# A substitution's rows loaded in four transfers of 32 partitions, a scheduler's DMA prices, and another admission order

## The chip, the cores and the metric

The kernel runs on one core of a Trainium2 chip. The core's engines are TensorE (PE; its weight loads are shown apart as PEld), VectorE (DVE), ScalarE (ACT), GpSimd (POOL) and SyncE (SP), which here issues every DMA of the kernel. Each engine works through its own list of instructions in order and waits on semaphores for the others. The metric is device time in microseconds (us), from three executions, with one more execution under the profiler.

## The reference

One decoder layer: a prompt of 2048 tokens and 8 single-token samples, model width 1024, everything in fp32. One input projection (1024 to 11280 columns) feeds a gated DeltaNet branch of 8 heads and a dilated attention branch of 12 heads; the branches are projected, gated, merged, projected again, normed and added to the input. What matters here is the chunked delta rule of the DeltaNet branch:

```
a_mat = jnp.where(strict, jnp.einsum('bnhcd,bnhed->bnhce', kb, k) * decay, 0.0)
u = solve(v * beta[..., None])             # (I + a_mat) u = rhs, a_mat strictly lower
w = solve(kb * jnp.exp(G)[..., None])
...
v_new = u_c - w_c @ S ; o_c = qd_c @ S + qk_c @ v_new ; S = S * gl_c + kd_c.T @ v_new   # per chunk
```

For each head and each chunk a triangular system is solved; then a state S runs from chunk to chunk.

## The kernel before, in words

The prompt is worked in two halves of 1024 tokens. In each half a main task on TensorE computes the input projection, 128 columns after another, as a block-recursive product with split operands (tiles `xs*`, `xp*` against weights `wh`, `wl`; L241 issues every matmul, L257 every transpose). Its partial sums are combined in PSUM by `to_c` and `to_d` (L974, L979), which add a bank and `etmp` on VectorE; TensorE waits for these sums. In between run the heads' tasks: short convolutions (`convw`), attention pairs, and for each of the 8 DeltaNet heads of a half the function `inverse` (L1295) and a loop over 8 chunks in `gdn` (L1150). A turn of that loop goes back and forth between TensorE and VectorE: `rr` from a product with the state `st`, `ww`, and the new `st` (the rows `rr<-bank`, `ww<-bank`, `st<-st,teGl,bank`).

`inverse` runs 16 times. The system of a head lies in a page (`at`). Its diagonal blocks of 32 x 32 are stored to DRAM (`wl_d`, four stores), and read back so that each partition holds a whole block's rows, 1024 numbers; the same 32 rows of 4 KB go to each of four groups of 32 partitions. This is `lane_w`. A second load brings the identity into `lane_t`. Then VectorE runs the substitution: 31 steps of a product (`lane_x<-lane_w,lane_t`) and a sum (`lane_t<-lane_t,lane_x`). The result goes to DRAM and back (`tl`), and products on TensorE complete the inverse. There is one set of lane buffers.

```
1307    yield K.load(wp, bass.AP(tensor=wd.tensor, offset=wd.offset, ap=[[0, 4], [1024, 32], [1, 1024]]))
1308    yield K.load(tp, I["c_consts"][:, CONST_T:])
```

No order of instructions is written down. All tasks are generators that yield operations; the class `Scheduler` keeps a clock for each engine and a table of when each buffer is written and read, and issues next the operation that can start first by its own prices (`issue`). So a price changes where every later instruction stands on its engine. A DMA is priced in `issue` (L149) by its bytes over a rate, behind the DMA that was issued before it, and `load` (L386) gives the bytes. The strings `ORDER` (L2104) say in which order the column tiles of each half are worked and admitted to the 17 pages: G adds a head's k, q and v tiles, Z its gate, a an attention tile group, g a merge gate; the other letters admit single pieces of work.

Of the kernel before, what the change touches and what calls it, by code (L numbers as in the profile page):

```python
# [86 lines left out]
class Scheduler:  # L87
# [54 lines left out]
    def issue(self, op, alt, start):  # L142
        eng, cost, fn = alt
        fn()
        end = start + cost
        self.clock[eng] = end
        self.busy[eng] += cost
        if op.nbytes:
            self.dma = max(self.dma, end + 650.0) + op.nbytes / 360.0  # L149
            end = self.dma  # L150
            eng = "dma"
        bufs = self.bufs
        for n in op.reads:
            b = bufs.setdefault(n, [0.0, 0.0, None, None])
            if end > b[1]:
                b[1], b[3] = end, eng
        for n in op.writes:
            b = bufs.setdefault(n, [0.0, 0.0, None, None])
            if end > b[0]:
                b[0], b[2] = end, eng  # L160
# [40 lines left out]
def _names(*aps):  # L201
    return tuple(a.tensor.name for a in aps if isinstance(a, bass.AP))


def _free(ap):
    n = 1
    for x in ap.shape[1:]:
        n *= x
    return n


class Ops:
# [10 lines left out]
    def mm_cost(self, out, lhsT, rhs):  # L223
        n = _free(rhs)
        if lhsT.dtype == F32R:
            return max(n / 2.215, 107.0)
        k, m = lhsT.shape[0], _free(lhsT)
        floor = 214.0 if m > 64 else (125.0 if m > 32 else 77.0)
        return max(n * 1.68, floor)
# [31 lines left out]
    def act_alt(self, out, in_, func, scale=1.0, bias=0.0, accum_out=None):  # L261
        nc = self.nc
        c = _free(in_) / 1.2 + (51.0 if self.in_psum(in_) else 93.0)
        c += 93.0 * (isinstance(scale, bass.AP) + isinstance(bias, bass.AP) + (accum_out is not None))
        if accum_out is not None and func == AF.Square:
            c += 130.0
        kw = dict(scale=scale, bias=bias)
        if accum_out is not None:
            kw["accum_out"] = accum_out
        return ("act", c, lambda: nc.scalar.activation(out, in_, func, **kw))  # L270
# [115 lines left out]
    def load(self, out, in_):  # L386
        nc = self.nc
        n = 4 * _free(out) * out.shape[0]
        return Op([("sp", 475.0, lambda: nc.sync.dma_start(out, in_))], _names(in_), _names(out), nbytes=n)  # L389


# [51 lines left out]
def build(nc, tc, ctx, I, O):  # L443
# [7 lines left out]
    K = Ops(nc, {b.tensor.name for b in banks})  # L451
# [698 lines left out]
    def gdn(hf, h, tk, tq, tv, tz, work, done):  # L1150
# [43 lines left out]
        for u in range(2):  # L1194
# [8 lines left out]
            side.release(b)  # L1203
        U_ev, Q_ev, V_ev = Event(), Event(), Event()
        S.spawn(inverse(at, U_ev), 11, f"inv{h}")
        S.spawn(gdn_q(tq, kT, e, gp, sm, tb, h, Q_ev), 12, f"gq{h}")
        qT, qk = yield Wait(Q_ev)
# [87 lines left out]
    def inverse(at, ev):  # L1295

        i = gidx[0] % 3
        gidx[0] += 1
        wd, td = wl_d[i], tl_d[i]
        a3 = at[:, :HT].rearrange("p (n c) -> p n c", c=128)  # L1300
        wv = wd.rearrange("(n b) (j i) -> b j n i", b=4, i=32)
        for b in range(4):
            yield K.load(wv[b], a3[32 * b:32 * b + 32, :, 32 * b:32 * b + 32])

        ln = yield Acquire(lanes, 1)
        wp, tp, xp = ln
        yield K.load(wp, bass.AP(tensor=wd.tensor, offset=wd.offset, ap=[[0, 4], [1024, 32], [1, 1024]]))
        yield K.load(tp, I["c_consts"][:, CONST_T:])
        W = wp.rearrange("p (j i) -> p j i", i=32)
        Tm = tp.rearrange("p (c i) -> p c i", i=32)  # L1310
        for j in range(31):
            m = 31 - j
            x = xp[:, :8 * m].rearrange("p (c i) -> p c i", i=m)
            yield K.tt(x, W[:, j, None, j + 1:].to_broadcast([128, 8, m]),
                       Tm[:, :, j, None].to_broadcast([128, 8, m]), OP.mult)
            yield K.tt(Tm[:, :, j + 1:], Tm[:, :, j + 1:], x, OP.add)
        yield K.load(td, tp)
        lanes.release(ln)
        tb, pt = yield Acquire(prob_t, 2)
        TB = tb.rearrange("p (n c) -> p n c", c=64)  # L1320
        Uv = a3
        yield K.pset(TB[0:32, :, 32:64], 0.0)
        tv = td.rearrange("(q n b) (c i) -> b q c n i", q=4, b=4, i=32)
        for b in range(4):
            for q in range(4):
                r = 32 * b + 8 * q
                yield K.load(Uv[r:r + 8, :, 32 * b:32 * b + 32], tv[b, q])
        for b in range(4):
            yield K.vtr(TB[32 * b:32 * b + 32, :, 32 * (b % 2):32 * (b % 2) + 32],
                        Uv[32 * b:32 * b + 32, :, 32 * b:32 * b + 32])  # L1330
        P1 = pt[:, :256].rearrange("p (n c) -> p n c", c=32)
        bank = yield Acquire(side, 1)
        b1 = bank[:, :256].rearrange("p (n c) -> p n c", c=32)
        b2 = bank[:, 256:].rearrange("p (n c) -> p n c", c=32)
        for a in range(2):
            lo, hi = slice(64 * a, 64 * a + 32), slice(64 * a + 32, 64 * a + 64)
            yield K.mms([(b1[hi, n], a3[lo, n, 64 * a + 32:64 * a + 64], TB[lo, n, 0:32], True, True)
                         for n in range(8)])
            yield K.copy(P1[hi], b1[hi])
        yield K.mms([(b2[32:64, n], Uv[32:64, n, 32:64], P1[32:64, n], True, True) for n in range(8)])  # L1340
        for a in range(2):
            lo, hi = slice(64 * a, 64 * a + 32), slice(64 * a + 32, 64 * a + 64)
            yield K.mms([(b2[lo, n], P1[hi, n], Uv[hi, n, 64 * a + 32:64 * a + 64], True, True) for n in range(8)])
        yield K.copy(TB[32:64, :, 0:32], b2[32:64])
        for a in range(2):
            lo = slice(64 * a, 64 * a + 32)
            yield K.copy(Uv[lo, :, 64 * a + 32:64 * a + 64], b2[lo])
        side.release(bank)
        bank = yield Acquire(side, 1)
        b1 = bank.rearrange("p (n c) -> p n c", c=64)  # L1350
        yield K.mms([(b1[64:128, n], a3[0:64, n, 64:128], TB[0:64, n], True, True) for n in range(8)])
        P2 = pt.rearrange("p (n c) -> p n c", c=64)
        yield K.copy(P2[64:128], b1[64:128])
        yield K.mms([(b1[0:64, n], P2[64:128, n], Uv[64:128, n, 64:128], True, True) for n in range(8)])
        yield K.copy(Uv[0:64, :, 64:128], b1[0:64])
        side.release(bank)
        prob_t.release(tb, pt)
        ev.set(at)
# [731 lines left out]
    def conv_state():  # L2090
# [10 lines left out]
    plan, admits = [], []  # L2101


    ORDER = ("GZaaGaaGZaagZGaZagGZaagGagZaGaZaggGaZaggggggxgggyg",  # L2104
             "gGZgaagGagZSaggGaZaGagZagGaagTZGaZaCgggGaaZgGZaggag")
    for hf in range(2):
        tiles = []

# [45 lines left out]

        for what in ORDER[hf]:
            if what in "GZag":
# [5 lines left out]
            else:  # L2162
                ev, n = {"S": (sg_admit, 4), "T": (sat_admit, 3), "C": (cs_admit, 1)}[what]
# [101 lines left out]
def trace(nc, arrays):  # L2265
    from contextlib import ExitStack

    ins = {n: nc.dram_tensor(f"in_{n}", a.shape, mybir.dt.from_np(a.dtype), kind="ExternalInput").ap()
           for n, a in arrays.items()}
    outs = [nc.dram_tensor(f"out_{i}", s, F32, kind="ExternalOutput").ap() for i, s in enumerate(_OUTS)]  # L2270
    with tile.TileContext(nc) as tc, ExitStack() as ctx:
        return build(nc, tc, ctx, ins, outs)
# [13 lines left out]
```

## Time and profile before

| | |
|---|---|
| median of 3 executions | 3112.87 us (3108.63 to 3118.22) |
| profiled execution | 3111.94 us, span of its instructions 3110.2 us |
| mean granted TensorE clock | 0.988 |
| PE busy | 3028.9 us, 97% of the span |
| DVE busy | 2193.5 us, 71% |
| ACT busy | 1218.4 us, 39% |
| DMA queue of SP | 331.49 MB, 36.3% of 16 engines' time |

PE is busy nearly all the time, so a change in this kernel is read from what interrupts PE: an idle stretch and what ended it, and the granted clock, which is shown as a share of 2.4 GHz and has the two levels 1.0 and 0.5. A wait is put down to the instruction or the DMA that came last before it ended.

### The profile page before, as it was taken

What the parts mean: (1) busy time and instruction counts of PE and PEld (TensorE: products, weight loads), DVE (VectorE), ACT (ScalarE), POOL (GpSimd) and SP (SyncE); (2) the same over time, 40 slices, a digit from 0 to 9 for tenths busy, and PEclk for the clock granted to TensorE, in tenths of its full rate; (3) what the DMA queues carried; (4) which work ended last, traced back from release to release, by engine and by line L of the source; (5) the groups of instructions that cost most, each with busy time, mean ns of one, the idle gap of its engine ahead of it and who ended that gap; (6) DMA issues with size and microseconds to landing.
All of it is one profiled execution on the core that took longest, in us unless ns stands there. A gap on an engine that the chain in (4) does not pass through costs nothing.

```text
span 3110.2 us, 55704 instructions
## 1 busy us (share of the span) xinstructions
PE 3028.9 (97%) x20879; PEld 2702.7 (87%) x20879; DVE 2193.5 (71%) x5975; ACT 1218.4 (39%) x3427; POOL 131.0 (4%) x237
## 2 busy tenths in 40 slices
PE   7999999989999999999999999999999999999999
PEld 6999999989999999978877778888888888898887
DVE  6767866776868478666676757686978686766765
ACT  4544444434444343433433434343424443222121
POOL 1000000000000000000000000000000000000000
PEclk9999999999999999999999999999999999999999
DMA  4222232232323225322233232236453225565463
GB/s 120 77 66 80 68 88 82 81 88 67 89 72 86 73 87 150 105 72 79 71 100 107 80 107 85 81 90 181 138 146 99 77 75 160 170 227 191 140 238 115
DMA packets 434135, 335.06 MB, mean 108 GB/s; under 512 B 62313, under 2 KB 377201, under 8 KB 433856
## 3 DMA queue, kind: packets, MB, share of 16 engines
q1 hardware_dynamic: 433864, 331.49, 36.3%
q8 instruction: 164, 2.69, 0.4%
q14 instruction: 107, 0.88, 0.1%
HBM read 253.01 MB, written 80.97 MB: 107 GB/s over the span
## 4 chain that ended last, share of the span: by engine, by line
PE 82%; DVE 8%; DMA 8%; SPq 1%; issue 1%; ACT 1%; POOL 0%; DVEq 0%; POOLq 0%; ACTq 0%
PE bank L241 78%; PE bank L257 4%; DMA lane_t<-in_c_consts 3%; DVE pg L301 2%; SPq L389 1%; DVE wl L306 1%; DMA pg<-og 1%; DVE lane_x L306 1%; DVE lane_t L306 1%; DMA wr<-in_w_in 1%; DMA pg<-sq_d 1%; DMA pg<-in_state_gdn 1%; DMA wl<-pg 0%; DVE pg L306 0%; DVE wh L345 0%
## 5 line engine op out<-in xcount | busy, mean ns | idle before, releaser
L270 ACT ACTIVATE pg<-bank 128x256 f32<-128x256 f32 (+8 forms) x755 | 341.5, 465 | 762.9 <-PE bank L241 681.5
L306 DVE TENSOR_TENSOR wl<-wr,wh 128x512 fp32r<-128x512 f32 x595 | 383.7, 647 | 20.6 <-ACT wh L270 3.6
L241 PE MATMUL bank<-xp7s,wh 128*128 128x512 f32 (+3 forms) x1196 | 305.4, 330 | 0.0
L345 DVE CAST wh<-wr 128x512 fp32r<-128x512 f32 (+1 forms) x377 | 150.3, 399 | 219.0 <-PE bank L241 195.0
L241 PE MATMUL bank<-xp6s,wh 128*128 128x512 f32 (+3 forms) x1132 | 289.0, 331 | 0.0
L270 ACT ACTIVATE wh<-wr 128x512 fp32r<-128x512 f32 (+1 forms) x220 | 134.2, 611 | 382.9 <-PE bank L241 325.0
L241 PE MATMUL bank<-xp5s,wh 128*128 128x256 f32 (+3 forms) x1100 | 278.4, 330 | 0.0
L241 PE MATMUL bank<-xp4s,wh 128*128 128x260 f32 (+2 forms) x1068 | 267.5, 327 | 0.0
L306 DVE TENSOR_TENSOR bank<-bank,etmp 128x256 f32<-128x256 f32 (+2 forms) x260 | 134.8, 519 | 135.7 <-PE bank L241 132.0
L241 PEld LDWEIGHTS bank<-xp7s,wh 128*128 128x128 f32 x1196 | 199.8, 189 | 17.3 <-issue 1.5
L241 PEld LDWEIGHTS bank<-xp6s,wh 128*128 128x128 f32 (+1 forms) x1132 | 188.9, 188 | 17.0 <-DVE xp6s L301 0.2
L241 PEld LDWEIGHTS bank<-xp5s,wh 128*128 128x128 f32 (+1 forms) x1100 | 183.3, 189 | 15.3 <-issue 0.8
L241 PE MATMUL bank<-xp7s,wl 128*128 128x512 f32 (+3 forms) x592 | 195.7, 331 | 0.0
L241 PEld LDWEIGHTS bank<-xp4s,wh 128*128 128x128 f32 x1068 | 176.1, 188 | 14.2 <-issue 1.5
L306 DVE TENSOR_TENSOR lane_x<-lane_w,lane_t 128x248 f32<-128x248 f32 (+30 forms) x496 | 141.8, 286 | 64.3 <-DMA lane_t<-in_c_consts 58.2
L241 PE MATMUL bank<-xp6s,wl 128*128 128x512 f32 (+2 forms) x560 | 185.9, 332 | 0.0
L301 DVE SCALAR_TENSOR_TENSOR pg<-pg,convw,pg 128x1024 f32<-128x1024 f32 x144 | 184.0, 1278 | 1.9 <-issue 0.5
L241 PE MATMUL bank<-xp5s,wl 128*128 128x512 f32 (+2 forms) x544 | 178.5, 328 | 0.0
L241 PE MATMUL bank<-xs1k,wh 128*128 128x512 f32 (+4 forms) x708 | 178.1, 335 | 0.0
L241 PE MATMUL bank<-xs6k,wh 128*128 128x512 f32 (+3 forms) x680 | 174.3, 335 | 0.3 <-DVE xs6k L306 0.3
L241 PE MATMUL bank<-xp4s,wl 128*128 128x256 f32 (+2 forms) x528 | 173.7, 329 | 0.0
L241 PE MATMUL bank<-xs7k,wh 128*128 128x512 f32 (+3 forms) x680 | 172.3, 335 | 0.0
(297 smaller groups left out, 7428.4 us busy)
## 6 DMA issues: line engine op xcount, KB each, us to landing
wr<-in_w_in SPq DMA_DIRECT2D x176, 512.0 KB
pg<-in_x_prompt SPq DMA_DIRECT2D x32, 512.0 KB
wr<-in_w_proj_a SPq DMA_DIRECT2D x32, 512.0 KB
wr<-in_w_out SPq DMA_DIRECT2D x32, 512.0 KB
pg<-og SPq DMA_DIRECT2D x24, 520.0 KB
pg<-gate SPq DMA_DIRECT2D x24, 512.0 KB
out<-pg SPq DMA_DIRECT2D x20, 512.0 KB
og<-pg SPq DMA_DIRECT2D x32, 260.0 KB
```

Of the source, the lines that this page charges most:

```text
L241: nc.tensor.matmul(out, lhsT, rhs, start=start, stop=stop, skip_group_check=shared)
L257: nc.tensor.transpose(out, in_, ident[:k, :k])
L270: return ("act", c, lambda: nc.scalar.activation(out, in_, func, **kw))
L301: lambda: nc.vector.scalar_tensor_tensor(out, in0, scalar, in1, op0=op0, op1=op1, **kw))],
L306: return ("dve", self._vcost(out, in0, in1), lambda: nc.vector.tensor_tensor(out, in0, in1, op=op))
L345: alts.append(("dve", self._vcost(out, in_, fast=True), lambda: nc.vector.tensor_copy(out, in_)))
L389: return Op([("sp", 475.0, lambda: nc.sync.dma_start(out, in_))], _names(in_), _names(out), nbytes=n)
```

## The change

Three edits. The load of `lane_w` becomes four loads of 32 partitions, each with the plain 32 x 1024 source. The scheduler's price of a DMA goes from 360 to 270 bytes per nanosecond, and a transfer whose contiguous runs on both sides hold at least 512 numbers has its bytes counted at 0.72 (270 / 0.72 = 375). The two strings that admit tiles are changed at some places.

```
-            self.dma = max(self.dma, end + 650.0) + op.nbytes / 360.0
+            self.dma = max(self.dma, end + 650.0) + op.nbytes / 270.0
...
+def _run(ap):
+    run = 1
+    for step, n in reversed(list(ap.ap)[1:]):
+        if step != run:
+            break
+        run *= n
+    return run
...
         n = 4 * _free(out) * out.shape[0]
+        n *= 0.72 if min(_run(out), _run(in_)) >= 512 else 1.0
...
-        yield K.load(wp, bass.AP(tensor=wd.tensor, offset=wd.offset, ap=[[0, 4], [1024, 32], [1, 1024]]))
+        for q in range(4):
+            yield K.load(wp[32 * q:32 * q + 32], wd)
         yield K.load(tp, I["c_consts"][:, CONST_T:])
...
-    ORDER = ("GZaaGaaGZaagZGaZagGZaagGagZaGaZaggGaZaggggggxgggyg",
+    ORDER = ("GZaaGaaZGaagZGaZagGaZagGagZaGaZgaggGgaZaggggxggygg",
```

The second string of `ORDER` has one pair of letters exchanged. PE, DVE, ACT and POOL get the same work as before; SP gets 1353 DMAs where it had 1305.

SP's list at the fifth of the sixteen inversions (the fifth head of the first half), before. `wl_163` is the DRAM tile with the head's blocks, `wr_*` are the two buffers for weights, `grow` is a row of decays:

```order
L389 DMA pg_98<-grow_158 128x1024
L389 DMA snew_d<-pg_106 128x8
L389 DMA wl_163<-pg_100 32x8x32 x2
L389 DMA wr_113<-in_w_in 128x8x128
L389 DMA wl_163<-pg_100 32x8x32
L389 DMA wr_112<-in_w_in 128x8x128
L389 DMA wl_163<-pg_100 32x8x32
L389 DMA lane_w<-wl_163 128x1x1024
L389 DMA lane_t<-in_c_consts 128x256
```

The same place in the change:

```order
L400 DMA pg_100<-grow_158 128x1024
L400 DMA wl_163<-pg_101 32x8x32 x2
L400 DMA snew_d<-pg_110 128x8
L400 DMA wl_163<-pg_101 32x8x32 x2
L400 DMA lane_w<-wl_163 32x1024
L400 DMA wr_113<-in_w_in 128x8x128
L400 DMA wr_112<-in_w_in 128x8x128
L400 DMA lane_w<-wl_163 32x1024 x3
L400 DMA lane_t<-in_c_consts 128x256
```

One load has become four, the identity's load stands behind all four, and at this place two weight loads stand between the first and the other three.

DVE's list at the start of the same substitution, before (`lane_x<-lane_w,lane_t` is its first product; `bank_68<-bank_66,etmp` is a sum of the projection, `pg_99<-pg_104,pg_99` the end of a convolution):

```order
L301 SCALAR_TENSOR_TENSOR pg_99<-pg_104,pg_99 128x1024
L306 TENSOR_TENSOR bank_68<-bank_66,etmp 128x256
L301 SCALAR_TENSOR_TENSOR st_146<-st_146,teGl,bank_72 128x128
L301 SCALAR_TENSOR_TENSOR rr<-bank_72,tneG,pg_110 128x128
L345 COPY ww<-bank_72 128x128
L301 SCALAR_TENSOR_TENSOR st_146<-st_146,teGl,bank_72 128x128
L306 TENSOR_TENSOR lane_x<-lane_w,lane_t 128x248
L306 TENSOR_TENSOR lane_t<-lane_t,lane_x 128x8x31
L301 SCALAR_TENSOR_TENSOR rr<-bank_72,tneG,pg_110 128x128
```

The same place in the change:

```order
L316 TENSOR_TENSOR bank_68<-bank_66,etmp 128x256
L311 SCALAR_TENSOR_TENSOR rr<-bank_69,tneG,pg_98 128x128
L355 COPY ww<-bank_69 128x128
L311 SCALAR_TENSOR_TENSOR st_146<-st_146,teGl,bank_69 128x128
L301 TENSOR_SCALAR sm_141<-sm_141 128x8
L311 SCALAR_TENSOR_TENSOR pg_99<-bank_71,ghh,pg_99 128x512
L311 SCALAR_TENSOR_TENSOR rr<-bank_69,tneG,pg_98 128x128
L311 SCALAR_TENSOR_TENSOR pg_103<-bank_70,sm_141,pg_103 128x128 x2
L311 SCALAR_TENSOR_TENSOR st_146<-st_146,teGl,bank_69 128x128
L311 SCALAR_TENSOR_TENSOR pg_103<-bank_70,sm_141,pg_103 128x128
L316 TENSOR_TENSOR lane_x<-lane_w,lane_t 128x248
L311 SCALAR_TENSOR_TENSOR pg_103<-bank_70,sm_141,pg_103 128x128
```

Behind the same sum `bank_68<-bank_66,etmp` the first product stood after the end of one turn of the chunk loop and one whole turn; now it stands after two whole turns and, on the way, five other instructions. Over the sixteen inversions DVE's list has on the mean 20 instructions between the last one that writes the head's system and the first product before, and 35 in the change.

## Rows read from the trace of the kernel before

**Rows 1.** Page, part 1: busy time, share of the span, instructions.

```profile
PE 3028.9 (97%) x20879; PEld 2702.7 (87%) x20879; DVE 2193.5 (71%) x5975; ACT 1218.4 (39%) x3427; POOL 131.0 (4%) x237
```

**Rows 2.** Waits of PE: total us, times, longest us.

```profile
PE bank L241 <- DVE rr L301: 17.7, 8, 8.6
PE bank L241 <- DMA cst<-in_c_consts: 11.3, 1, 11.3
```

**Rows 3.** Tile lane_w: duration ns min/median/max, first and last start; idle time before.

```profile
L306 DVE TENSOR_TENSOR lane_x<-lane_w,lane_t x496: 157/283/419, 135.5 to 2575.3; 128x248 f32<-128x248 f32 x6, 128x224 f32<-128x224 f32 x6, 128x200 f32<-128x200 f32 x6, 128x176 f32<-128x176 f32 x6
L389 SPq DMA_DIRECT2D lane_w<-wl x16: 539/573/621, 125.0 to 2527.1; - x16
...
  DMA lane_t<-in_c_consts: 58.2, 13
```

**Rows 4.** Timeline, DVE, fifth inversion: start us, us, instruction, [idle before <- releaser].

```profile
663.24 0.35 DVE L301 SCALAR_TENSOR_TENSOR st<-st,teGl,bank 128x128 f32<-128x128 f32 x1 [0.64 <-PE bank L241]
672.38 0.42 DVE L306 TENSOR_TENSOR lane_x<-lane_w,lane_t 128x248 f32<-128x248 f32 x1 [8.80 <-DMA lane_t<-in_c_consts]
...
673.17 0.34 DVE L301 SCALAR_TENSOR_TENSOR rr<-bank,tneG,pg 128x128 f32<-128x128 f32 x1
```

**Rows 5.** Timeline, PE, behind six starts of a substitution.

```profile
143.63 0.51 PE L241 MATMUL bank<-xs5k,wh 128*128 128x260 f32 x2 [2.81 <-DVE bank L306]
...
260.64 0.79 PE L241 MATMUL bank<-st,pg 128*128 128x128 f32 x2 [6.14 <-DVE st L301]
...
673.57 0.80 PE L241 MATMUL bank<-rr,pg 128*128 128x128 f32 x2 [8.56 <-DVE rr L301]
...
957.83 0.79 PE L241 MATMUL bank<-rr,pg 128*128 128x128 f32 x2 [5.45 <-DVE rr L301]
...
1750.83 3.54 PE L241 MATMUL bank<-pg,pg 128*128 128x2 f32 x16 [5.66 <-DMA pg<-in_state_gdn]
...
2053.19 0.49 PE L241 MATMUL bank<-rr,pg 128*128 128x128 f32 x2 [1.10 <-DVE rr L301]
```

**Rows 6.** Timeline, SP: start us, us until issued, DMAs; fifth, eighth, thirteenth inversion.

```profile
659.98 0.57 SPq L389 DMA_DIRECT2D lane_w<-wl  x1
660.60 0.47 SPq L389 DMA_DIRECT2D lane_t<-in_c_consts  x1
...
1130.59 1.80 SPq L389 DMA_DIRECT2D wl<-pg  x4
1133.72 0.58 SPq L389 DMA_DIRECT2D lane_w<-wl  x1
...
2041.77 12.37 SPq L389 DMA_DIRECT2D wr<-in_w_in  x2
```

**Rows 7.** Windows: stretch, us, busy by engine, granted clock, DMA share, GB/s.

```profile
2.00:7.00 5.00, 0.00 (x0) 0.00 (x0) 2.46 (x4) 1.28 (x1) 0.00 (x0) 1.00 0.96 343
...
534.70:538.70 4.00, 4.00 (x37) 4.00 (x36) 2.60 (x6) 2.90 (x15) 0.00 (x0) 1.00 0.26 84
1137.00:1141.00 4.00, 4.00 (x36) 4.00 (x36) 1.03 (x4) 2.06 (x11) 0.00 (x0) 1.00 0.25 80
```

**Rows 8.** Windows: PE first; stretches at the lower granted clock, each with the next.

```profile
258.30:265.10 6.80, 4.46 (x21) 4.46 (x22) 3.50 (x11) 0.21 (x1) 0.00 (x0) 0.50 0.07 24
265.10:272.00 6.90, 6.90 (x61) 6.90 (x61) 6.55 (x24) 2.91 (x13) 1.28 (x3) 1.00 0.05 12
667.90:678.10 10.20, 4.53 (x21) 4.54 (x22) 3.80 (x12) 1.63 (x8) 0.00 (x0) 0.50 0.62 95
678.10:688.30 10.20, 10.20 (x88) 10.20 (x88) 9.87 (x38) 3.38 (x12) 1.01 (x1) 1.00 0.41 121
...
1749.90:1760.10 10.20, 9.27 (x34) 8.43 (x35) 8.06 (x23) 0.00 (x0) 0.00 (x0) 0.50 0.01 3
1760.10:1770.30 10.20, 10.20 (x51) 8.31 (x50) 8.66 (x24) 6.06 (x10) 0.00 (x0) 1.00 0.24 64
```

More of the change, by code (lines that the diff above doesn't have):

```diff
@@ L2101, in build @@
     plan, admits = [], []
-    ORDER = ("GZaaGaaGZaagZGaZagGZaagGagZaGaZaggGaZaggggggxgggyg",
-             "gGZgaagGagZSaggGaZaGagZagGaagTZGaZaCgggGaaZgGZaggag")
+    ORDER = ("GZaaGaaZGaagZGaZagGaZagGagZaGaZgaggGgaZaggggxggygg",
+             "gGZaaggGagSaZggGaZaGagZagGaagTZGaaZCgggGaaZgGZaggag")
     for hf in range(2):
```

## The prediction

> **What bounds the kernel now.** I read the page's busy times first: PE is busy for 3028.9 of 3110.2 us [rows 1], so 81.3 us of its idle time are all that a change of order can give back, besides time in which PE runs at the lower clock. Next I asked what PE waits for. The largest wait with one cause is for `rr`, the row of the chunk loop that VectorE makes from PE's product, 17.7 us in 8 times [rows 2]. A row of 0.35 us cannot hold PE up for 8.6 us by itself, so the third question is what kept VectorE. The view of `lane_w` tells it: VectorE stood idle for 58.2 us in 13 times at the first product of a substitution, waiting for its loads [rows 3]. At the fifth inversion the order of events is plain. `st` ends at 663.6, the next row in VectorE's list is the first product, it begins at 672.38 after 8.80 us of idleness, and `rr` stands behind it, at 673.17 [rows 4]; PE goes on at 673.57, after 8.56 us [rows 5]. VectorE is no bound by its work (71% busy [rows 1]); it is in order, and what stands behind the waiting product is what PE needs.
>
> PE's stretches of this kind are six that I can follow: 2.81, 6.14, 8.56, 5.45, 5.66 and 1.10 us, together 29.7 [rows 5]. The first is a delay passed on (the sum in `bank` came late because VectorE began late); in the fifth PE waits for a load of `in_state_gdn` that was issued behind a `lane_w`. After four of them PE runs at granted clock 0.50, which is 1.2 GHz, for 6.8 to 10.2 us, then at 2.4 GHz again [rows 8]. What that costs I take from the work done: behind the second wait 21 matmuls took 4.46 us, and in the stretch after it 61 took 6.90, so 21 would take 2.4 and 2.1 are lost; behind the third 21 took 4.53 against 88 in 10.20, again 2.1 lost; behind the fifth 34 took 9.27 against 51 in 10.20, 2.5 lost. The fourth is like the second (1.8). Sum 8.5 us; the mix of matmuls differs between such stretches, so it is an estimate, good to some 3 us.
>
> Why are the loads late? `lane_w` was issued at 659.98 [rows 6] and was needed at 663.6, and the product began 12.4 us after the issue. Its 512 KB move slowly: in two stretches with hardly anything else under way the DMA engines are busy for 0.26 and 0.25 of their time and move 84 and 80 GB/s, while the loads of `in_x_prompt` at the start, 128 partitions of the same 4 KB rows, fill 0.96 and move 343 GB/s [rows 7]. A quarter of 16 engines is four, and four is the outer count of the load's pattern (`[0, 4]`). At 82 GB/s the 512 KB take 6.4 us, at 343 they take 1.5. The scheduler priced them at 1.5 us, and so it put the product where it had to wait. Others suffer too: two weight loads behind a `lane_w` took 12.37 us to be issued [rows 6].
>
> **The change part by part.** *The four transfers.* Each has 32 partitions outermost, rows of 4 KB. No row of before shows just this form. Bounds: it is as fast as the 128-partition load (343 GB/s), or as slow as `lane_w` was. I take the first, since the two loads differ in the outer count alone and each fits the engines it could use; halfway between would change little, as will be seen. Readiness from the first issue: four issues at 0.573 us [rows 3] and the identity's at 0.47 [rows 6] are 2.8 us, and behind the last issue there is a tail. For the tail the nearest row is that of the four stores to `wl`: the last is issued by 1132.39 and the load that waits for them starts at 1133.72, 1.3 us [rows 6]. I take 2.0 for a larger transfer, so 4.8 us in place of 12.4 at the fifth inversion, and of 10.5 at the first (125.0 to 135.5 [rows 3]).
>
> A rule of the Trainium skill speaks against this edit: "DMA: Bandwidth & Descriptors", section Rules for kernel authors, says of two transfers to disjoint partition halves that they are not worth it, since both use all 16 engines anyway, and that one 128-partition transfer is better. By that rule the time to readiness would only grow by three issues, 1.7 us, and the gain would be what the new order covers (the third rival below). The same section says that an outermost dimension below 16, a zero-stride broadcast for one, confines a DMA to that many engines; the trace agrees, with 0.25 and 0.26 of the engines' time [rows 7].
>
> *The place of the product.* Over the sixteen inversions there are 35 instructions on VectorE in place of 20 between the last one that writes the system and the first product. An instruction takes 3110.2 / 5975 = 0.52 us of VectorE's span [rows 1], so the product stands some 7.8 us later, with useful work ahead of it. Either alone, the faster load (by 5.7 us or more) or the later place, would take most of 58.2 us; with both I expect under 5 us left. What is late next? The inverse itself ends later by what the product was moved (7.8 us) less the wait that is gone (58.2 / 16 = 3.6), some 4 us a head. That costs nothing as long as PE has projection matmuls to run, and it has: outside of such waits it hardly idles [rows 1, 2].
>
> *The issues.* 48 more at 0.573 us are 27.5 us on SP, 1.7 us an inversion. Queued behind them are weight loads and the identity. Cover: the weights are loaded one column pair ahead, and no row of PE's waits names a weight. If the cover were gone at every inversion, it would cost up to 27.5 us; I take 0.
>
> *The prices and the strings.* They add and remove no work; PE gets the same matmuls. They shuffle what remains: 81.3 less the 29.7 and less 11.3 us at the start, before the constants have landed [rows 2], is 40 us of idleness for other reasons. A quarter of it either way, 10 us, is the range I give to luck; its middle is 0.
>
> *The sum.* 3111.9 (the profiled execution) less 29.7, less 8.5, is 3073.7. That execution was 0.9 us under the median of the three, so on the median's scale the forecast is 3075 us. Bounds: 3056 if the other idleness falls by 10 us and its clock losses by some 9 with it; 3102 if the issues uncovered cost 27.5.
>
> **The rivals.** *Half is given back.* The waits of these places go, and others of the 40 us kind grow, or some issues are uncovered: 3075 plus half of the 38.2 us, 3094. For it: an in-order kernel at 97% has little slack, and every instruction has moved. Against it: the six waits had one cause that is taken away, whatever the order.
>
> *The transfers are no faster* and only the order helps. Then readiness is 1.7 us later and the product 7.8 later, a relief of 6.1 us. Of the six waits 2.5 us of the third stay, and all 5.66 of the fifth, which comes from a load stuck behind `lane_w`; with two of four clock losses (4.6) that is 12.8 us kept, 3088. The rule quoted above would give this case.
>
> *No change:* what is gained at these places is lost again whole, 3104 to 3122. For it: 40 us of idleness have causes that I have not followed, and the admission order touches all of them.
>
> *Slower,* by one mechanism. SP is in order, and at the fifth inversion the list of the change puts two weight loads between the first part of `lane_w` and the other three. Such a load waits until its buffer has been split on VectorE; if it waits long, so do three parts, the identity, and the substitution, and with it the page of the head; PE then stops at the products that need the inverse. To eat the 38.2 us and end 9.3 us over before, this must cost PE (38.2 + 9.3) / 16 = 3.0 us at every inversion. Against it: there are some 8 us of VectorE's work as new cover, and readiness has 5.7 us to spare.
>
> **How the numbers follow.** I take 9.3 us (0.3%) as what a measurement of this kernel can tell from no change: the three executions of before lie within 9.6. Chances: the forecast (3060 to 3084, below 3060 included) 0.62, half given back (3084 to 3103) 0.17, transfers no faster (about 3088) 0.06, no change 0.09, slower 0.06. The first three are faster by over 0.3%: 0.85. The range of 8 in 10 leaves out the last two cases, 0.15, and a little at the low end: 3056 to 3102. The likeliest case's own range is 3060 to 3084.
>
> **What would show it.** Right: VectorE's idle time at `lane_x` falls from 58.2 to under 5 us; readiness from the first `lane_w` issue is about 5 us; DMA share right behind those issues is far over 0.25; PE's wait for `rr` falls from 17.7 to under 5 us, and the stretches at 0.50 behind substitutions are gone, so that the mean granted clock is over 0.99; PE's busy time falls by some 8 us and its idleness to about 52. Wrong: if VectorE still waits as long at `lane_x`, the transfers or their place on SP are to blame; if it does not wait there and PE is idle for 80 us all the same, the order gave it back, and the view of PE's waits names where.

## The result and the profile after

The changed kernel takes 3060.47 us (median of 4 runs, 3055.23 to 3061.43); the kernel before, run beside it, 3110.75 us (3107.09 to 3118.22). The ratio is 0.9832, with a 95% interval of 0.9809 to 0.9854: 50 us faster, where 38 were forecast. The direction and the range held, but the time lies at the lower edge of the likeliest case (3060 to 3084); two terms of the sum were too small.

The span of the profiled execution is 3059.6 us, the mean granted clock 0.992. The page's busy times, to be held against [rows 1]:

```profile
PE 3018.4 (99%) x20879; PEld 2698.0 (88%) x20879; DVE 2204.1 (72%) x5957; ACT 1216.7 (40%) x3443; POOL 131.2 (4%) x239
```

PE does the same 20879 matmuls. Its busy time is 10.5 us less, and its idle time is 3059.6 - 3018.4 = 41.2 us in place of 81.3, so 40.1 less. Together these are the 50.6 us by which the span is shorter.

The view of PE's waits after, against [rows 2] (total us, times, longest us):

```profile
PE bank L267 <- DVE pg L316: 11.5, 5, 6.4
PE bank L251 <- DMA cst<-in_c_consts: 10.3, 1, 10.3
PE bank L251 <- DVE rr L311: 1.9, 4, 1.0
```

The wait for `rr` is down from 17.7 to 1.9 us. A wait that was not among the rows of before now leads. It is for pages that VectorE writes with an elementwise operation (TENSOR_TENSOR, L316, which is L306 in the kernel before); the longest of the five, 6.4 us, stands at 35.0 us, where the kernel before waits 4.6 us for a load of `in_a_log`, and the other four stand near 1293. More of it under the experiments. The tile `lane_w` after, against [rows 3]:

```profile
L316 DVE TENSOR_TENSOR lane_x<-lane_w,lane_t x496: 163/285/419, 138.2 to 2529.4; 128x248 f32<-128x248 f32 x6, 128x224 f32<-128x224 f32 x6, 128x200 f32<-128x200 f32 x6, 128x176 f32<-128x176 f32 x6
L400 SPq DMA_DIRECT2D lane_w<-wl x64: 312/421/2547, 124.8 to 2479.6; - x64
its engine sat idle before it (us, times) until:
who waited for it (us, times):
```

There are 64 loads in place of 16, with a median issue of 0.421 us against 0.573, and the list of what VectorE waited for ahead of a product is empty: 58.2 us in 13 times became nothing. At the fifth inversion, against [rows 4], VectorE does not wait at the first product, and `rr` follows 0.6 us behind it:

```profile
666.76 0.35 DVE L311 SCALAR_TENSOR_TENSOR st<-st,teGl,bank 128x128 f32<-128x128 f32 x1
667.02 0.35 DVE L311 SCALAR_TENSOR_TENSOR pg<-bank,sm,pg 128x128 f32<-128x128 f32 x1
667.28 0.41 DVE L316 TENSOR_TENSOR lane_x<-lane_w,lane_t 128x248 f32<-128x248 f32 x1
667.61 0.34 DVE L311 SCALAR_TENSOR_TENSOR pg<-bank,sm,pg 128x128 f32<-128x128 f32 x1
667.87 0.34 DVE L311 SCALAR_TENSOR_TENSOR rr<-bank,tneG,pg 128x128 f32<-128x128 f32 x1
```

SP's timeline of the same inversion, against [rows 6] (start, us until issued, DMAs):

```profile
652.17 0.32 SPq L400 DMA_DIRECT2D lane_w<-wl  x1
652.87 3.42 SPq L400 DMA_DIRECT2D wr<-in_w_in  x2
656.34 2.06 SPq L400 DMA_DIRECT2D lane_w<-wl  x3
658.44 0.42 SPq L400 DMA_DIRECT2D lane_t<-in_c_consts  x1
```

Two weight loads did stand between the first part and the other three, for 3.42 us, and the identity was issued 6.3 us after the first part. The product at 667.28 comes 15.1 us after the first issue, and the product did not wait. The windows view, with the columns of [rows 7], shows the speed of the four transfers (ahead of two substitutions), two stretches at a lower granted clock, and the second place of the new wait:

```profile
239.80:241.30 1.50, 1.50 (x48) 1.46 (x46) 0.17 (x1) 1.20 (x2) 0.00 (x0) 1.00 0.90 249
2479.50:2481.00 1.50, 1.50 (x12) 1.34 (x10) 0.90 (x3) 0.94 (x1) 0.00 (x0) 1.00 0.91 265
...
375.00:381.80 6.80, 6.40 (x30) 5.86 (x29) 5.87 (x13) 3.28 (x9) 0.40 (x1) 0.52 0.01 2
388.00:394.80 6.80, 6.24 (x29) 5.84 (x30) 5.85 (x17) 3.65 (x15) 1.01 (x1) 0.53 0.84 218
1293.00:1303.20 10.20, 7.19 (x28) 5.57 (x29) 9.71 (x28) 3.37 (x6) 0.00 (x0) 0.50 0.35 83
```

The share of the engines is 0.90 and 0.91 in the first two, where one load alone had 0.25 and 0.26. In the last PE works for 7.19 of 10.20 us, at granted clock 0.50, which is 1.2 GHz. The stretches at 375 and 388 us are new: from 340 to 420 us the granted clock is 0.91 here and 1.00 in the kernel before.

### The profile page after: what moved, and what is told of

Same layout as the page of the kernel before. It is cut to its first block, busy times and chain, and to the rows that moved or that the text cites. A ratio compares the mean times of both kernels' runs of the same rounds, so it can differ in the third digit from the quotient of the medians.

```text
span 3059.6 us, 55757 instructions
## 1 busy us (share of the span) xinstructions
PE 3018.4 (99%) x20879; PEld 2698.0 (88%) x20879; DVE 2204.1 (72%) x5957; ACT 1216.7 (40%) x3443; POOL 131.2 (4%) x239
## 4 chain that ended last, share of the span: by engine, by line
PE 94%; DVE 4%; DMA 1%; issue 1%; ACT 1%; POOL 0%; SPq 0%; DVEq 0%; POOLq 0%; ACTq 0%
PE bank L251 89%; PE bank L267 5%; DVE pg L311 1%; DVE wl L316 0%; DVE lane_t L316 0%; DVE lane_x L316 0%; DVE pg L316 0%; DVE junk L311 0%; DMA pg<-in_x_prompt 0%; DMA wr<-in_w_in 0%; DMA ghh<-in_g_head_norm 0%; DMA pg<-gate 0%; DVE wh L355 0%; ACT L280 0%; ACT pg L280 0%
## 5 line engine op out<-in xcount | busy, mean ns | idle before, releaser
L280 ACT ACTIVATE pg<-bank 128x256 f32<-128x256 f32 (+5 forms) x738 | 333.9, 464 | 746.0 <-PE bank L251 676.9
L316 DVE TENSOR_TENSOR wl<-wr,wh 128x512 fp32r<-128x512 f32 x595 | 384.0, 647 | 20.1 <-ACT wh L280 2.2
L316 DVE TENSOR_TENSOR bank<-bank,etmp 128x256 f32<-128x256 f32 (+2 forms) x260 | 135.0, 519 | 138.3 <-PE bank L251 133.4
L251 PEld LDWEIGHTS bank<-xp6s,wh 128*128 128x128 f32 (+1 forms) x1132 | 189.0, 188 | 18.2 <-issue 1.5
L251 PEld LDWEIGHTS bank<-xp5s,wh 128*128 128x128 f32 (+1 forms) x1100 | 182.9, 188 | 15.1 <-issue 0.8
L280 ACT ACTIVATE prob<-bank 128x512 f32<-128x512 f32 (+4 forms) x221 | 102.6, 478 | 189.0 <-PE bank L251 116.2
```

Source lines behind the costliest of these rows:

```text
L251: nc.tensor.matmul(out, lhsT, rhs, start=start, stop=stop, skip_group_check=shared)
L316: return ("dve", self._vcost(out, in0, in1), lambda: nc.vector.tensor_tensor(out, in0, in1, op=op))
```

## The experiments

The theory was that the slow load held VectorE up, and with it PE, so that the speed of the load alone should give most of the gain. The rival was that the other order, made by the prices, the strings and the four operations, gave it by putting the product later or by moving something else. All ratios are to the kernel before on the same chip, with 95% intervals. Edits are against the kernel before unless a heading says otherwise.

**e1, the fast load in the old order.** One operation for the scheduler, with the old price, issues four transfers. The lists of PE, VectorE, ScalarE and GpSimd are then those of before, row for row; SP alone has 48 issues more.

```
+    def parts(self, pairs):
+        nc = self.nc
+        n = sum(4 * _free(o) * o.shape[0] for o, _ in pairs)
+        def go():
+            for o, i in pairs:
+                nc.sync.dma_start(o, i)
+        return Op([("sp", 475.0, go)], _names(pairs[0][1]), _names(pairs[0][0]), nbytes=n)
...
-        yield K.load(wp, bass.AP(tensor=wd.tensor, offset=wd.offset, ap=[[0, 4], [1024, 32], [1, 1024]]))
+        yield K.parts([(wp[32 * q:32 * q + 32], wd) for q in range(4)])
```

> The kernel before with its lists for PE, DVE, ACT and POOL unchanged row for row; only the one lane_w load on SP is issued as four of 32 partitions. Theory (the load was slow because its outer count is 4, and the faster load removes the waits by itself): readiness about 5 us after the first issue in place of 10.5 to 13.6, DVE's idle time at lane_x from 58.2 to under 6 us, time about 3075 us, a gain of 30 to 45. Rival (transfers no faster, the new order is what helped): DVE still idle for over 50 us there, time 3108 to 3140, the three more issues included.

Measured: 3057.47 us (3049.92 to 3060.85), ratio 0.9823 [0.9805, 0.9841]. The whole gain is there without a price or a string changed; the expected 3075 was too high, as the forecast was. The page's busy times, the tile `lane_w`, SP's timeline and VectorE's at the fifth inversion, one fence each:

```profile
PE 3009.4 (99%) x20879; PEld 2689.8 (88%) x20879; DVE 2193.8 (72%) x5975; ACT 1219.8 (40%) x3427; POOL 132.4 (4%) x237
```

```profile
L392 SPq DMA_DIRECT2D lane_w<-wl x64: 312/420/1512, 124.2 to 2467.1; - x64
...
  DMA lane_t<-in_c_consts: 5.3, 4
```

```profile
648.27 1.70 SPq L392 DMA_DIRECT2D lane_w<-wl  x4
650.01 0.42 SPq L398 DMA_DIRECT2D lane_t<-in_c_consts  x1
```

```profile
652.73 0.42 DVE L306 TENSOR_TENSOR lane_x<-lane_w,lane_t 128x248 f32<-128x248 f32 x1 [0.99 <-DMA lane_t<-in_c_consts]
```

The product starts as soon as its loads have landed, 652.73 - 648.27 = 4.5 us after the first issue, where one load took 12.4. PE idles for 3048.1 - 3009.4 = 38.7 us. Since the lists are equal, any wait of PE that is gone is gone by the load's speed.

**e8, e1 once more,** to know how firm it is.

> The lists of before with the load in four transfers, once more, beside the changed kernel. Theory (the new prices and strings give nothing beyond the load): within 0.3% of the changed kernel, 3050 to 3064. Rival (they cost, since the substitution is put 7 us later without need): 5 us or more below the changed kernel. Second rival (the first run of it was lucky): 5 us or more above it, as the forecast's 3075 would have it.

Measured: 3053.19 us (3050.64 to 3054.13), 0.9821 [0.9801, 0.9841]; VectorE idle at `lane_x` for 3.7 us in 4 times.

**e2, the slow load in the new order** (against the changed kernel): its lists are kept, but the first of the four operations issues the old load of all 128 partitions, and the other three issue nothing.

```
-            yield K.load(wp[32 * q:32 * q + 32], wd)
+            op = K.load(wp[32 * q:32 * q + 32], wd)
+            whole = bass.AP(tensor=wd.tensor, offset=wd.offset, ap=[[0, 4], [1024, 32], [1, 1024]])
+            go = (lambda: K.nc.sync.dma_start(wp, whole)) if q == 0 else (lambda: None)
+            op.alts = [("sp", 475.0, go)]
+            yield op
```

> The change with its lists for PE, DVE, ACT and POOL unchanged row for row; SP issues the old single load at the place of the first of the four, and nothing at the other three. In the trace after, the first product begins 12.4 to 23.7 us behind that place, the old load is ready after 9.5 to 13.8. Theory (either the faster load or the later place takes the waits away): DVE idle at lane_x under 12 us, time 3060 to 3080. Rival (the slow load also harms what stands behind it on the 16 engines and on SP, wherever the product stands): DVE does not wait at lane_x, but other loads are late, time 3080 to 3100.

Measured: 3073.42 us (3071.35 to 3074.69), 0.9872 [0.9854, 0.989]. The new order alone gives 40 us on this chip (3113.08 before), so either part alone takes most of the wait: VectorE idles for 1.3 us in 2 times. What stays is the harm to others. The lists of the four compute engines are those of the changed kernel, so what is longer here, beyond scatter, is so by the load. PE's waits in e2:

```profile
PE bank L251 <- DMA pg<-in_state_gdn: 5.9, 1, 5.9
PE bank L251 <- DVE bank L316: 4.9, 2, 3.8
```

The load of `in_state_gdn` is late again, by about as much as in [rows 5], where the changed kernel has no wait at all, and one wait for `bank` is longer by 3.8 us. e2 is 16 us over e1 on the same chip.

**e3, e1 with two transfers of 64 partitions:**

```
+        yield K.parts([(wp[64 * q:64 * q + 64], bass.AP(tensor=wd.tensor, offset=wd.offset, ap=[[0, 2], [1024, 32], [1, 1024]]))
+                       for q in range(2)])
```

> As the first run of this call, lists of before unchanged on four engines, but the load is two transfers of 64 partitions, each with the outer count 2 in its source pattern. Theory (the outer count sets how many engines move a load): two engines, DMA share near 0.13 and some 42 GB/s with nothing else under way, readiness 6 us and more later than before, DVE idle at lane_x well over 120 us, time over 3170. Rival (a load is slow for its repeated source or for its size, and smaller transfers are faster): readiness between that of four and of one transfer, time 3075 to 3112.

Measured: 3188.6 us (3185.42 to 3192.79), 1.0243 [1.0224, 1.0263], slower than before. Splitting in itself brings nothing here; the outer count decides. Three stretches with little but these transfers under way, in the windows view:

```profile
365.00:373.00 8.00, 8.00 (x74) 7.79 (x74) 5.13 (x13) 4.75 (x21) 0.00 (x0) 1.00 0.13 41
...
854.00:860.00 6.00, 6.00 (x53) 6.00 (x53) 4.48 (x12) 2.23 (x14) 0.00 (x0) 1.00 0.12 43
...
552.00:558.00 6.00, 6.00 (x53) 6.00 (x52) 4.42 (x10) 3.15 (x18) 0.00 (x0) 1.00 0.13 51
```

An outer count of two gives half the share (0.12 to 0.13) and about half the rate of four. The wait grows with it, on VectorE (tile `lane_w`) and from there on PE (its waits):

```profile
  DMA lane_t<-in_c_consts: 123.9, 15
```

```profile
PE bank L241 <- DVE rr L301: 37.4, 9, 12.8
PE bank L241 <- DVE bank L306: 28.2, 10, 7.2
```

**e9, the four loads alone.** Four operations for the scheduler, with the old prices and strings, so that the lists differ a little from before.

```
-        yield K.load(wp, bass.AP(tensor=wd.tensor, offset=wd.offset, ap=[[0, 4], [1024, 32], [1, 1024]]))
+        for q in range(4):
+            yield K.load(wp[32 * q:32 * q + 32], wd)
```

> The kernel before with four lane_w loads that the scheduler sees as four operations, at the old prices and with the old strings, so that the lists move as the scheduler decides. Theory (the load is all of the gain): 3050 to 3066 us, DVE idle at lane_x under 8 us. Rival (four operations on SP at old prices put the product or the weights at worse places): 3070 to 3095.

Measured: 3059.99 us (3057.56 to 3062.86), 0.9847 [0.9833, 0.986]; VectorE idles for 0.4 us at `lane_x`, once.

**e4, the change without its strings.**

```
-    ORDER = ("GZaaGaaZGaagZGaZagGaZagGagZaGaZgaggGgaZaggggxggygg",
-             "gGZaaggGagSaZggGaZaGagZagGaagTZGaaZCgggGaaZgGZaggag")
+    ORDER = ("GZaaGaaGZaagZGaZagGZaagGagZaGaZaggGaZaggggggxgggyg",
+             "gGZgaagGagZSaggGaZaGagZagGaagTZGaZaCgggGaaZgGZaggag")
```

> The change with the ORDER strings of before: four transfers and the new prices. Theory (the strings only shuffle; the load and its price are the gain): 3060 to 3080, DVE idle at lane_x under 5 us. Rival (the part of the gain that the forecast did not have, some 12 us, comes from the strings): 3070 to 3080 with the further idle time of PE back in the second half; or more than that, 3085 and over, if the strings carry more.

Measured: 3062.92 us (3058.67 to 3065.84), 0.9838 [0.9819, 0.9857]; VectorE idles for 1.2 us at `lane_x`, in 2 times.

**e5, the strings alone** (those two lines of the change, the one slow load).

> The kernel before with the ORDER strings of the change alone: one lane_w load of 128 partitions, old prices. Theory (the whole gain comes from the load): DVE still idle for 45 to 70 us at lane_x, time 3100 to 3125, no difference that can be told. Rival (the strings carry part of the 50 us): 3070 to 3100.

Measured: 3121.09 us (3114.23 to 3131.0), 1.004 [1.0028, 1.0052]. VectorE waits for 60.9 us in 11 times at `lane_x`, against 58.2 in 13. The time lies in the range of the theory, but its "no difference that can be told" failed: the interval leaves out 1.

**e6, the prices alone** (360 to 270, and 0.72 with `_run`; the one slow load).

```
-            self.dma = max(self.dma, end + 650.0) + op.nbytes / 360.0
+            self.dma = max(self.dma, end + 650.0) + op.nbytes / 270.0
...
+        n *= 0.72 if min(_run(out), _run(in_)) >= 512 else 1.0
```

> The kernel before with the new prices alone (270, and 0.72 for long runs): one lane_w load, which is priced at 375 bytes per ns in place of 360, old strings. Theory (the prices do not know of the outer count, so the product stays where it is): DVE idle at lane_x 45 to 70 us, time 3100 to 3125. Rival (dearer short runs move the substitution or the weights enough): DVE idle under 40 us, time 3070 to 3100.

Measured: 3097.06 us (3090.67 to 3106.61), 0.9963 [0.9949, 0.9977]; 45.6 us in 11 times at `lane_x`. The idle time is as the theory had it, the time as its rival. With the slow load the strings cost 12 us and the prices bring 12.

**e7, the changed kernel again,** on the chip of e5, e6 and e8.

> The changed kernel once more, to stand on the same chip as the next run. 3055 to 3066 us; the same shape as in its first profile, no DVE idle time at lane_x.

Measured: 3056.83 us (3053.46 to 3059.75), 0.9834 [0.9813, 0.9855].

**e10, the fast load as one operation with the new prices,** old strings: e1 and the edit of e6 together.

> Four transfers issued as one operation of the scheduler, with the new prices and the old strings: the order that the prices alone give, with the fast load. The prices alone gave 12 us without it. If these 12 us are of another kind than the load's, this is the fastest version, 3040 to 3050 us; if they came from putting waits elsewhere that the fast load removes as well, 3050 to 3064, no better than the changed kernel.

Measured: 3050.64 us (3041.43 to 3056.21), 0.9815 [0.9793, 0.9837], the lowest of all. Its interval overlaps those of e1, e8 and the change, so that it beats them is not shown. Against e9 on the same chip it is 9 us faster, and each of its 4 times is below each of the 5 of e9; the two differ in the prices and in the number of operations, and which of them does it was not tried.

What follows from the ten: with the fast load, the five kernels that differ in prices, strings and operations per load (e1 and e8, e9, e4, e10, the change) lie between 0.9815 and 0.9847, and their intervals overlap: the load is the gain, and the rest moves these medians by 10 us at most. With the slow load the prices and strings are worth some 12 us each, in opposite directions. In the profile the new prices have one visible cost. Every kernel that has them (the change, e2, e4, e6, e7, e10) shows PE waiting 10.0 to 12.5 us in 5 times for pages that VectorE writes at L316; 6.1 to 6.4 us of that are the wait at 35 us. Without the prices PE waits 4.6 to 4.8 us there, for `in_a_log`. So the prices cost some 1.5 us at the start. The rest, 3.9 to 6.4 us, stands near 1300 us (the windows row at 1293 is part of it); without the prices it is 3.0 to 3.1 us in e1, e3, e5, e8 and before, but 5.8 in e9, so that the prices are not shown to be what makes it longer.

## Why the prediction was right, and where its sizes were off

**The mechanism** (one in-order engine held by a slow load, and PE behind it) is shown by e1: nothing on the four compute engines was moved, the load was made faster, and the gain came whole.

**The speed of the four transfers.** The prediction took the rate of the 128-partition load with no row for it. The changed kernel's 0.90 of the engines' time and 249 GB/s, in a stretch that holds the beginnings and ends of the transfers too, put it on the side of that bound (343) and far from the other (82); what the sum needed, the time to readiness, came out as said below.

The rule that was weighed against this edit ("DMA: Bandwidth & Descriptors" of the Trainium skill, section Rules for kernel authors, on two transfers to disjoint partition halves) takes for granted that one transfer already uses all 16 engines. Here that didn't hold, and e1 shows a gain where the rule alone would give none. Where two transfers to disjoint halves were run, each with an outer count of two (e3), the engines were busy for 0.12 to 0.13 of their time. The other row of the same section, that a small outermost count confines a DMA to so many engines, agrees with shares of 0.12 to 0.13 for two, 0.25 to 0.26 for four and 0.90 for 32.

**Readiness** was put at 4.8 us from the first issue; e1 has 4.5 where VectorE waits for it. In the changed kernel it can't be read, as no product waits. VectorE's idle time at `lane_x` was put under 5 us and is 0. That either half alone would take most of the wait holds too: 5.3 us stay in e1 and 1.3 in e2.

**One reading was wrong, without weight in the sum.** The 12.37 us that two weight loads took to be issued were put down to the `lane_w` ahead of them. In e1, behind the fast load, the same two loads at the thirteenth inversion still take 8.68 us (1993.93 in SP's timeline), so at most 3.7 us were the load's.

**The first term that was mis-sized** is "PE's stretches of this kind are six that I can follow ... together 29.7". PE's idle time fell by 40.1 us in the changed kernel and by 42.6 in e1. The prediction had set 40 us aside as "idleness for other reasons" with a middle of 0. In equal pieces of work (the same matmuls, within three, on PE in each), the windows view of before and then of e1:

```profile
0.00:1300.00 1300.00, 1254.71 (x11018) 1236.08 (x11019) 922.49 (x2620) 584.62 (x1808) 67.74 (x136) 0.99 0.31 87
1300.00:2684.00 1384.00, 1354.82 (x7779) 1118.75 (x7778) 994.71 (x2856) 540.40 (x1433) 52.17 (x84) 0.99 0.37 105
2684.00:3110.20 426.20, 419.39 (x2087) 347.92 (x2085) 276.31 (x501) 93.38 (x186) 11.12 (x17) 1.00 0.52 178
```

```profile
0.00:1271.60 1271.60, 1247.64 (x11018) 1228.79 (x11019) 922.07 (x2620) 585.34 (x1808) 67.76 (x136) 1.00 0.31 89
1271.60:2622.30 1350.70, 1342.66 (x7781) 1113.41 (x7781) 995.39 (x2856) 541.02 (x1433) 53.54 (x84) 0.99 0.38 108
2622.30:3048.10 425.80, 419.07 (x2084) 347.58 (x2082) 276.36 (x501) 93.41 (x186) 11.14 (x17) 1.00 0.53 179
```

The span less PE's busy time is its idleness. In the first piece it falls from 45.3 to 24.0 us, by 21.3, where the four stretches that the prediction counted there hold 22.96. In the second it falls from 29.2 to 8.0, by 21.2, where the prediction counted 5.66 and 1.10. So 14.4 us were missed, all in the second piece; in the last nothing changes (6.8 to 6.7). Compared matmul by matmul, what vanished besides are first of all six waits of 0.4 to 2.4 us, together 9.1, that stand 12 to 24 us behind a waiting product and name an ordinary instruction of VectorE; a seventh, of 0.8, stands 7.5 us behind one. Two more, of 0.5 and 0.7, stand right behind a product, like those that the prediction counted. The 3.3 us left are spread over waits that were not followed. Four of the six, first VectorE's timeline of before at the product ahead of two of them, then PE's:

```profile
1563.27 0.42 DVE L306 TENSOR_TENSOR lane_x<-lane_w,lane_t 128x248 f32<-128x248 f32 x1 [6.23 <-DMA lane_t<-in_c_consts]
```

```profile
1575.14 0.74 PE L241 MATMUL bank<-xs5k,wh 128*128 128x512 f32 x2 [1.46 <-DVE bank L306]
...
1585.07 0.66 PE L257 MATMUL bank<-cst,pg 128*128 128x128 f32 x4 [1.81 <-DVE pg L301]
...
1946.62 0.66 PE L257 MATMUL bank<-cst,pg 128*128 128x128 f32 x4 [2.23 <-DVE pg L301]
...
2438.62 0.66 PE L257 MATMUL bank<-cst,pg 128*128 128x128 f32 x4 [2.44 <-DVE pg L301]
```

and the windows of before between three such products and the last wait behind each:

```profile
1563.27:1585.00 21.73, 18.14 (x81) 13.85 (x79) 21.45 (x52) 8.68 (x17) 0.00 (x0) 1.00 0.22 63
1925.80:1946.60 20.80, 18.59 (x88) 14.69 (x87) 20.29 (x47) 9.07 (x19) 0.00 (x0) 1.00 0.29 78
2415.26:2438.60 23.34, 20.16 (x95) 16.06 (x93) 22.96 (x59) 11.98 (x20) 0.00 (x0) 1.00 0.31 79
```

VectorE's busy time is the third of the busy columns: 21.45 of 21.73, 20.29 of 20.80, 22.96 of 23.34 us. It lost 6.23 us at the first of these products, 3.14 and 4.79 at the others, and had next to no idle time in which to make that up, so what PE next needed from it was late. The prediction followed each waiting product only to PE's next stop, 1 to 8 us behind it. VectorE is no bound over the whole span, yet in the second piece it is one for 20 us at a time.

**The second term that was mis-sized** is the lower clock, "Sum 8.5 us". PE's busy time fell by 10.5 us in the changed kernel, 18.2 in e7, which is the same kernel, 19.5 in e1 and 15.0 in e8, its twin. With two levels, the time at the lower one is twice the span times what the mean granted clock lacks of 1: before 2 x 3110.2 x 0.012 = 75 us, changed 2 x 3059.6 x 0.008 = 49, e7 (0.995 of 3053.0) 31, e1 (0.996 of 3048.1) 24; the rounding of the mean makes each good to some 3 us. The four stretches that the prediction took are 34 of the 75. Two that it missed stand behind the small waits at 1946.62 and 2438.62:

```profile
1948.00:1955.00 7.00, 7.00 (x41) 6.15 (x41) 6.27 (x25) 1.90 (x7) 0.00 (x0) 0.77 0.00 0
...
2439.00:2446.00 7.00, 7.00 (x29) 5.61 (x28) 6.28 (x24) 3.01 (x8) 0.00 (x0) 0.76 0.23 66
```

In e1, behind the same two products (1885 to 1915 and 2365 to 2395 us there), the granted clock is 1.00. The changed kernel has new ones in return, at 375 and 388 us, behind the first product of its third substitution (373.2), so the sign "the stretches at 0.50 behind substitutions are gone" came true only in part. How much goes in all differs between two executions of one kernel by 8 us of busy time, so this term can't be told more closely.

**The rivals.** That half is given back did not happen; what is seen of it are the 1.5 us at the start, 2 us more than before near 1293, and the two new stretches at the lower clock. "Transfers no faster" is shown false by e1, though its estimate of what the slow load would still cost, 12.8 us, stands close to what e2 has over the changed kernel (3073.42 - 3060.47 = 13.0 us, on two chips; by the ratios 12.4). That is in part luck: the wait for `in_state_gdn` is there as estimated (5.9 for 5.66 us), but the 4.6 us of clock losses are not, since PE's busy time is no longer (3017.7 against 3018.4 us), and other waits stand in their place. The rival that would have been slower is real as to its mechanism (3.42 us between the parts on SP) and is covered as the prediction said. The 48 issues cost nothing that can be measured: e1 has all of them and no wait of PE in it names a weight.

**What stays open** is why the prices gain and the strings lose 12 us with the slow load. VectorE's idle time at `lane_x` moves the right way (45.6 and 60.9 against 58.2 us), but by the strings only 2.7 us, and their other waits weren't followed.

## What to carry to other kernels

Read a DMA's rate from a stretch in which it is alone, and look at the outermost count of its pattern when the share of the engines is a simple fraction; here a replicated load split into one transfer per copy needed no other edit. When an in-order engine waits, ask how busy it is in the 20 us after: if it is full, as here, its wait can be paid by others further on, in small waits that name ordinary work. And when a change has a new order in it, run the one physical edit in the old order first: here that alone was the gain.

## What the runs showed of the hardware

Two transfers of 64 partitions with an outer count of two were slower than one of 128 with an outer count of four: 0.12 to 0.13 of the engines' time and 41 to 51 GB/s against 0.25 to 0.26 and 80 to 84, and the kernel lost 2.4% where the four of 32 gained 1.8%. An issue of a quarter load on SP took 0.42 us in the median, not the 0.573 of the whole one, so that the four issues of an inversion took 4 x 0.42 = 1.7 us where 4 x 0.573 = 2.3 were expected. Behind the slow load another load came late: PE waited 5.7 us (before) and 5.9 us (e2) for `in_state_gdn`, and with the fast load in the same two orders at most 0.4.
